# Output projection by seven block products: the large sums of its weights and operands on VectorE instead of GpSimd

## The chip, the cores and the metric

The kernel runs on one core of a Trainium2 chip. The metric is the device time of one execution in microseconds; of several executions the median is taken. The engines are named as in the profile: PE is TensorE (matmuls), DVE is VectorE, ACT is ScalarE, POOL is GpSimd, SP is SyncE, which only issues transfers here. A row of the profile reads: start, duration, engine, line, operation, output<-inputs, shape; in square brackets stands how long the engine idled ahead of it and what ended that.

## What is computed

One layer of a diffusion backbone on 1024 latent tokens of width 1024, with 256 context tokens. All is fp32.

```python
h_lat = rms_norm(x, norm1_g) * (1 + sc1) + sh1          # sh1, sc1, g1, ... from c @ w_mod
h_ctx = rms_norm(ctx, norm1_g) * (1 + csc1) + csh1
# one input projection, columns split into two head groups
(rq, rk, rv, rg), (dq, dk, dv) = split_heads(h @ w_in)
# retention, 4 heads, chunks of 128, in both directions, states carried from chunk to chunk
scores = einsum('bhid,bhjd->bhij', qc, kc) * intra
o = scores @ vc + (qc * q_dec) @ S
S = S * c_dec + (kc * k_dec).T @ vc
y_ret = silu(rg) * (group_norm(o_forward) + group_norm(o_backward))
# differential attention, 4 heads
y_diff = subln((softmax(q1 k1) - lam * softmax(q2 k2)) @ v)
x = x + g1 * (concat(y_ret, y_diff) @ w_out)            # the output projection
h2 = rms_norm(x, norm2_g) * (1 + sc2) + sh2
u = depthwise_conv3(h2 @ w_up) + conv_b
x = x + g2 * ((silu(a) * b) @ w_down)                   # a, b = halves of u
out = rms_norm(x, final_g)
```

## The kernel before

**Matmuls.** Every large product takes each operand as a high and a low part and makes three passes into one PSUM bank: high·high, high·low, low·high (`passes`, L133 to L135). So each operand is cast by ACT (the high part) and then DVE subtracts it from the original (the low part): `split_into` does that at L1333 and L1334, `split_op` at L1246 and L1247.

**What sets the order.** The code is handed to a scheduler that orders each engine's instructions by its own estimates; each engine then works strictly in that order. `in_order` pins stretches to the written order, and `tc.issue_after(i)` keeps an instruction behind instruction `i`. Work beside a product is written as a generator: `tick()`, called after each three matmuls, draws from `side` and from `along` at a given rate, starting at a given due value.

**Retention.** Beside the last columns of the input projection, `states_before` carries the backward states `Sb` from chunk to chunk (PSUM tile `pub`, DVE L249), and then `outputs()` takes 32 steps forward. A step makes the scores `sc`, the output `po` on PE (from `sc` and the states `Sf` and `Sb`), a copy `o` and its sums of squares `ss` on ACT, the power -0.5 of `ss` on POOL (L119, `rsqrt`), the product `o<-o,ss,gn` on DVE (L309), `y` from it on POOL (L311, L312), a turn of `y` on PE, and the next state `Sf` on DVE (L249). The PSUM tiles of these steps share three buffers (`pst`). `weight_blocks` runs along with it, one piece at a time: for each of four block columns `c` it loads two blocks of `w_out` (`w0x`, `w1x`, or the second half of the tile of `g1`, which the profile calls `g`), multiplies them by the gate `g1`, makes `t1` and a difference, and stores `t1_d`, `w2_d` and `w13_d` in DRAM (the tiles t1d, w2d, w13d of the profile).

**Attention.** Units of one head and one block of queries; a unit's keys `ks`, queries `qhl` and values `va` are loaded by POOL's queue. `first_weights` runs beside it: it loads gated weights (`woraw`) and retention outputs (`s<-yrd`, `y11o`) for the projection's first products.

**Output projection.** A product of 2 x 2 blocks by seven block products (Strassen's kind, with shared sums). Banks `oc`, `os`, `of` take products of four rows `r`, each of twelve matmuls (`out_product`); `to_x1` adds a bank to the residual `x1` on DVE (the tiles `x`, L1330). `oc` is used again on top of what it holds, so the next product into it must wait until DVE has read it. The operands: `t2 = w22 - t1` (L1360), `s2 += a` (L1372), `w21 -= t2` (L1377), each in pieces of 128x512 on POOL, and then `t2o`, `w22o`, `s1o`, `t1o`, ... as split operands. The sums `s2 += a` stand behind the last attention unit.

**After it.** `norm2` scales the rows `x1` (ACT square L1278, power on POOL, DVE scaling L1280); `turned` transposes them on PE (`pt`, L1286) for the up-projection, whose first weights are summed in place by `sums_in_place` (L1310 to L1312) on POOL, for two pairs of weights.

Of the kernel before, what the change touches and what calls it, by code (L numbers as in the profile page):

```python
# [8 lines left out]
F32 = mybir.dt.float32  # L9
# [3 lines left out]
ALU = mybir.AluOpType  # L13
# [46 lines left out]

TAIL = 2
GAP = 128
PREP_RATE, PREP_DUE = 0.4, -8.0
SPARE = (16, 4)
MOD_TICKS = 7
FIRST_LOADS = (22, 23, 25, 26, 28, 30)
# [5 lines left out]
def r32(ap):  # L72
    return ap.bitcast(F32)
# [3 lines left out]
def kernel(  # L77
# [16 lines left out]
    nc = tc.nc  # L94
# [22 lines left out]
    def rsqrt(out_ap, in_ap, mul, eps, n):  # L117
        nc.vector.tensor_scalar(out=out_ap, in0=in_ap, scalar1=mul, scalar2=eps, op0=ALU.mult, op1=ALU.add)
        return nc.gpsimd.tensor_tensor(out=out_ap, in0=out_ap, in1=mhalf[:, :n], op=ALU.pow).ins  # L119
# [29 lines left out]
    yr_d = [dr.tile([P, H, 2, 512], F32, name="yrd0"), dr.tile([P, H, 512], F32, name="yrd1")]  # L149
    t1_d = [dr.tile([P, 512], F32, name=f"t1d{c}") for c in range(4)]  # L150
# [9 lines left out]
    with ExitStack() as p1:  # L160
# [3 lines left out]
        raws = ExitStack()  # L164
# [77 lines left out]
        def dv_row(c):  # L242
            return dv_d[c * P : (c + 1) * P, :].rearrange("p (h e) -> p h e", e=P)

        def state_step(dst, prev, pu, h, d):
            if prev is None:
                nc.vector.tensor_copy(dst, pu)
            else:
                nc.vector.scalar_tensor_tensor(out=dst, in0=prev, scalar=cd[:, d * H + h : d * H + h + 1], in1=pu, op0=ALU.mult, op1=ALU.add)  # L249

        def load_step(n):
            h, t = divmod(n, NT)
# [161 lines left out]
        def weight_blocks():  # L414
            shared = rp.tile([P, 2, 2, 512], F32, name="g1", tag="rtab")
            g1 = shared[:, 0]
            nc.sync.dma_start(out=g1.rearrange("p n e -> p (n e)"), in_=g1_d)
            blocks = {}

            def load(c, i):  # L420
                t = blocks[c, i] = shared[:, 1] if c % 2 > i else er.tile([P, 2, 512], F32, name=f"w{i}x", tag="xhl")
                (nc.sync if c + i < 2 else nc.gpsimd).dma_start(out=t, in_=w_out[:, :, 4 * i + c, :].rearrange("n p e -> p n e"))

            def gated(t):
                nc.gpsimd.tensor_tensor(out=t, in0=t, in1=g1, op=ALU.mult)

            def kept(dst, o):
                nc.gpsimd.dma_start(out=dst, in_=o)

            load(0, 0)  # L430
            load(0, 1)
            for c in range(4):
                wa, wb = blocks[c, 0], blocks[c, 1]
                yield
                gated(wa)
                if c == 0:
                    load(1, 0)
                yield
                gated(wb)
                kept(w2_d[c], wb)  # L440
                yield
                t1 = er.tile([P, 512], F32, name="t1", tag=("xa", "xb")[c % 2])
                nc.gpsimd.tensor_tensor(out=t1, in0=wa[:, 1, :], in1=wa[:, 0, :], op=ALU.subtract)
                kept(t1_d[c], t1)
                yield
                nc.gpsimd.tensor_tensor(out=wa[:, 1, :], in0=wb[:, 1, :], in1=wa[:, 1, :], op=ALU.subtract)
                kept(w13_d[c], wa)
                for n, i in ((c + 1, 1), (c + 2, 0)):
                    if n < 4:
                        load(n, i)  # L450

        def natural(wget, lhs, tiles, finish):
            for t in tiles:
# [145 lines left out]
        with ExitStack() as p0:  # L599
# [70 lines left out]
            wget, load = stream_parts(2)  # L670
# [149 lines left out]
        er = p1.enter_context(tc.tile_pool(name="er", bufs=2, reuse_waits="tile"))  # L820
# [7 lines left out]
        cd = rc.tile([P, 8], F32, name="cd")  # L828
# [107 lines left out]
        n_units = NT * H  # L936
        units = {}
# [225 lines left out]
    raw_tiles = {}  # L1163

    def yraw(n, k):
        key = n, k // 2
        if key not in raw_tiles:
            raw_tiles[key] = opp.tile([P, 2, 512], F32, name=f"{n}{k // 2}", tag=f"r{PLACES[n] + k // 2}")
        return raw_tiles[key][:, k % 2, :]

    opb, later = {}, []
    u_ops, v_ops, a_ops = {}, {}, {}

    def first_weights():
        srcs = [(u_ops, "u", c, w13_d[c][:, 0, :]) for c in range(4)] + [(v_ops, "v", c, w2_d[c][:, 0, :]) for c in range(4)]
        raws = []
        for i in range(len(srcs) + 3):
            k = i // 2
            if i < len(srcs):
                if i % 4 == 0:  # L1180
                    yraw("s3", k)
                    nc.sync.dma_start(out=raw_tiles["s3", k // 2], in_=yr_d[1][:, k : k + 2])
                if i % 2 == 0:
                    a_ops[k] = op_tile("a", k, "y11o")
                    nc.gpsimd.dma_start(out=a_ops[k], in_=yr_d[0][:, k])
                raws.append(wrp.tile([P, 512], F32, name="woraw"))
                nc.sync.dma_start(out=raws[i], in_=srcs[i][3])
            if i >= 4 and i % 2 == 0:
                s3 = yraw("s3", k - 2)
                for a in range(2):  # L1190
                    part = r32(a_ops[k - 2][:, a, :])
                    later.append(dict(out=s3, in0=(part, s3)[a], in1=(s3, part)[a], op=(ALU.subtract, ALU.add)[a]))
            if i >= 3:
                ops, tag, c, _ = srcs[i - 3]
                o = ops[c] = op_tile(tag, c)
                nc.scalar.copy(o[:, 0, :], raws[i - 3])
                later.append(dict(out=o[:, 1, :], in0=raws[i - 3], in1=r32(o[:, 0, :]), op=ALU.subtract))
            yield
# [68 lines left out]
    x1 = [(x1lp if t < 4 else x1hp).tile([P, D], F32, name=f"x1_{t}") for t in range(NT)]  # L1267
    raw0 = rwp.tile([P, KD, 512], F32, name="raw0")
    sm2 = rwp.tile([P, 64], F32, name="sm2")

    def x1_load(ts):
        for t in ts:
            nc.sync.dma_start(out=x1[t], in_=x[t * P : (t + 1) * P, :])

    def norm2(t):
        nc.sync.dma_start(out=x1_d[t], in_=x1[t])
        sq = xo.tile([P, D], BF16, name="sq2")
        nc.scalar.activation(sq, x1[t], AF.Square, accum_out=sm2[:, t : t + 1])  # L1278
        power = rsqrt(sm2[:, t : t + 1], sm2[:, t : t + 1], 1.0 / D, EPS, 1)
        nc.vector.tensor_scalar(out=x1[t], in0=x1[t], scalar1=sm2[:, t : t + 1], scalar2=None, op0=ALU.mult)  # L1280
        return power

    def turned(hf, d, raw, on_act):
        pt = turn_tile[0]()
# [22 lines left out]
    def sums_in_place(a, b):  # L1307

        a1, a2, b1, b2 = a[:, 0:4, :], a[:, 4:8, :], b[:, 0:4, :], b[:, 4:8, :]
        nc.gpsimd.tensor_tensor(out=b1, in0=b1, in1=b2, op=ALU.add)  # L1310
        nc.gpsimd.tensor_tensor(out=a1, in0=b1, in1=a1, op=ALU.subtract)
        nc.gpsimd.tensor_tensor(out=a2, in0=a2, in1=a1, op=ALU.subtract)  # L1312

    C = 512
    left, right = slice(0, C), slice(C, D)
    with ExitStack() as p3:
# [25 lines left out]
        def raw_sums(n, tag):  # L1342
            o = [wop.tile([P, C], F32, name=n, tag=tag) for _ in range(4)]
            for k in range(4):
                nc.sync.dma_start(out=o[k], in_=dict(t1=t1_d[k], t3=w13_d[k][:, 1, :], w21=w2_d[k][:, 0, :], w22=w2_d[k][:, 1, :])[n])
            return o
# [9 lines left out]
        w22raw, t1raw = raw_sums("w22", "whi"), raw_sums("t1", "wlo")  # L1356
        x1_load(range(4))
        t2raw = [wop.tile([P, C], F32, name="t2", tag=("whi", "wlo")[k % 2]) for k in range(4)]
        for k in range(4):
            nc.gpsimd.tensor_tensor(out=t2raw[k], in0=w22raw[k], in1=t1raw[k], op=ALU.subtract)  # L1360
        chain = [psr.tile([P, C], F32, name=f"oc{r}", tag=f"c{r}") for r in (3, 0, 1, 2)]
        chain = chain[1:] + chain[:1]
        for r in range(4):
# [2 lines left out]
        with tc.issue_after(units[n_units - 1].exp_ins):  # L1366
            s2o = c_ops("s2")
        t2o = split_all("u", "t2o", t2raw)
        with tc.issue_after(units[n_units - 1].pool_ins.ins):
            for k in range(4):  # L1370
                for a in range(2):
                    nc.gpsimd.tensor_tensor(out=yraw("s2", k), in0=yraw("s2", k), in1=r32(a_ops[k][:, a, :]), op=ALU.add)  # L1372
        x1_load(range(4, NT))
        w22o = split_all("w", "w22o", w22raw)
        w21raw = raw_sums("w21", "whi")
        for k in range(4):
            nc.gpsimd.tensor_tensor(out=w21raw[k], in0=w21raw[k], in1=t2raw[k], op=ALU.subtract)  # L1377
        other = others("os")
        for r in range(4):
            out_product(other[r], r, opb, v_ops, True)  # L1380
# [29 lines left out]
        raws = [up_load(j) for j in range(NSUM)]  # L1410
# [106 lines left out]
    with ExitStack() as p4:  # L1517
# [143 lines left out]
        b0, b1 = Block(0), Block(1)  # L1661
# [16 lines left out]
        b2 = Block(2)  # L1678
# [30 lines left out]
        for j in range(3, NF):  # L1709
# [9 lines left out]
            last = blk  # L1719
# [32 lines left out]
    with ExitStack() as p5:  # L1752
# [255 lines left out]
```

## Time and profile before

| | |
|---|---|
| median of 3 runs | 1402.94 us (1401.28 to 1404.97) |
| profiled execution, its own time | 1398.59 us |
| its span | 1396.8 us |
| mean granted TensorE clock | 0.993 |
| PE busy | 1358.8 us (97%), 6980 matmuls |
| DVE busy | 1040.1 us (74%), 1492 instructions |
| ACT busy | 756.9 us (54%) |
| POOL busy | 434.3 us (31%), 445 instructions |

The span is the time from the first to the last instruction that the profile holds. A busy share is an average over stages that differ much; what an engine costs is read from the waits of a stage. A released wait is written as "PE oc L133 <- DVE x L1330": PE, about to write `oc`, waited for DVE's instruction on `x`.

### The profile page before, as it was taken

The numbers are of one execution on the slowest core, as the hardware profiler recorded it, in microseconds if no ns is written. First come the engines' busy times: TensorE is split into PE (matmuls) and PEld (weight loads), VectorE is DVE, ScalarE is ACT, GpSimd is POOL, SyncE is SP. The second block draws the span as 40 slices with busy tenths as digits, with TensorE's granted clock in tenths as the row PEclk, the third lists the DMA queues.
The fourth block names the chain that finished last, engine by engine and source line by source line (L and its number), as shares of the span: only waits on it lengthen the run. The fifth ranks groups of instructions, "written<-read, shape, count | busy, mean of one in ns | idle before, by whom it ended". The sixth has DMA issues, their size and how long they took to land.

```text
span 1396.8 us, 19720 instructions
## 1 busy us (share of the span) xinstructions
PE 1358.8 (97%) x6980; PEld 1139.5 (82%) x6980; DVE 1040.1 (74%) x1492; ACT 756.9 (54%) x1446; POOL 434.3 (31%) x445
## 2 busy tenths in 40 slices
PE   8999999999999899999899999999999999999997
PEld 6788888887888789998687878888888888788886
DVE  5867756634467888886778998887778777898756
ACT  5546444312466789997346745555445555455533
POOL 1310001566446334532704254223332220043003
PEclk9999999999999999999999999999999999999999
DMA  9467987898668494521514223322323226953324
GB/s 385 154 209 246 314 262 241 270 364 300 214 215 217 123 262 100 92 53 44 193 66 166 91 106 113 114 104 100 114 98 114 103 74 224 377 187 110 124 98 151
DMA packets 111242, 240.59 MB, mean 172 GB/s; under 512 B 10084, under 2 KB 42340, under 8 KB 109736
## 3 DMA queue, kind: packets, MB, share of 16 engines
q1 hardware_dynamic: 101320, 209.97, 44.0%
q0 software_dynamic: 9680, 29.10, 8.5%
q8 instruction: 55, 0.90, 0.3%
q14 instruction: 43, 0.35, 0.1%
q10 hardware_dynamic: 144, 0.26, 0.1%
HBM read 170.62 MB, written 68.42 MB: 171 GB/s over the span
## 4 chain that ended last, share of the span: by engine, by line
PE 59%; DMA 4%; DVE 3%; POOL 2%; issue 1%; ACT 1%; SPq 0%; POOLq 0%; DVEq 0%; ACTq 0%
PE chain L133 6%; PE chain L134 6%; PE chain L135 6%; PE pA L953 4%; PE pv L985 4%; PE c L135 4%; PE c L134 4%; PE c L133 4%; PE third L133 3%; PE third L134 3%; PE third L135 3%; PE pt L973 2%; DMA W<-w_down 2%; PE second L135 1%; PE second L134 1%; PE second L133 1%
## 5 line engine op out<-in xcount | busy, mean ns | idle before, releaser
L133 PE MATMUL pl<-hT,whi 128*128 128x512 f32 x256 | 107.6, 420 | 0.0
L1481 POOL TENSOR_TENSOR cmb<-wrb 128x512 f32<-128x512 f32 x20 | 31.1, 1555 | 236.8 <-DMA wrb<-w_up 182.2
L956 DVE TENSOR_REDUCE mt<-pA 128x1 f32<-128x1280 f32 x64 | 95.1, 1489 | 11.0 <-PE pA L953 10.5
L133 PE MATMUL chain<-T,whi 128*128 128x512 f32 x264 | 102.8, 389 | 0.0
L134 PE MATMUL chain<-T,whi 128*128 128x512 f32 x264 | 102.7, 389 | 0.0
L135 PE MATMUL chain<-T,wlo 128*128 128x512 f32 x264 | 102.7, 389 | 0.0
L135 PE MATMUL pl<-hT,wlo 128*128 128x512 f32 x256 | 100.5, 392 | 0.0
L134 PE MATMUL pl<-hT,whi 128*128 128x512 f32 x256 | 100.2, 391 | 0.0
L135 PE MATMUL c<-whi,ghl 128*128 128x512 f32 x232 | 90.4, 390 | 1.2 <-DVE ghl L1769 1.2
L953 PE MATMUL pA<-ks,qhl 128*128 128x512 f32 (+1 forms) x384 | 89.6, 368 | 1.4 <-DMA ks<-dk 1.4
L134 PE MATMUL c<-wlo,ghl 128*128 128x512 f32 x232 | 90.3, 389 | 0.0
L133 PE MATMUL c<-whi,ghl 128*128 128x512 f32 x232 | 90.3, 389 | 0.0
L960 ACT ACTIVATE p<-pA,mt 128x1280 f32<-128x1280 f32 x64 | 85.3, 1333 | 4.6 <-DVE mt L956 4.3
L133 PE MATMUL pn<-whi,hT 128*128 128x512 f32 x192 | 85.7, 446 | 0.2 <-ACT whi L201 0.2
L497 ACT ACTIVATE xb<-pl 32x512 f32<-32x512 f32 (+1 forms) x88 | 52.0, 590 | 61.0 <-PE pl L135 41.7
L1246 ACT CAST whi<-cmb 128x512 fp32r<-128x512 f32 x62 | 38.5, 622 | 77.3 <-PE chain L134 65.7
L953 PEld LDWEIGHTS pA<-ks,qhl 128*128 128x128 f32 x384 | 68.1, 190 | 13.0 <-issue 1.6
L135 PE MATMUL pn<-whi,hT 128*128 128x512 f32 x192 | 76.4, 399 | 1.0 <-POOL hT L662 1.0
L985 PE MATMUL pv<-va,aT 128*128 128x128 f32 x640 | 76.8, 275 | 0.0
L134 PE MATMUL pn<-wlo,hT 128*128 128x512 f32 x192 | 76.0, 396 | 0.8 <-DVE wlo L202 0.8
L985 PEld LDWEIGHTS pv<-va,aT 128*128 128x128 f32 x640 | 74.0, 192 | 0.4 <-ACT aT L979 0.3
L1246 ACT CAST whi<-wra 128x512 fp32r<-128x512 f32 x55 | 33.9, 621 | 70.8 <-PE third L134 43.5
(420 smaller groups left out, 4020.3 us busy)
## 6 DMA issues: line engine op xcount, KB each, us to landing
raw<-w_in SPq DMA_DIRECT2D x32, 512.0 KB, 5.6
wm<-w_mod SPq DMA_DIRECT2D x32, 512.0 KB, 4.8
wra<-w_up SPq DMA_DIRECT2D x24, 512.0 KB, 3.3
wrb<-w_up SPq DMA_DIRECT2D x23, 512.0 KB, 3.4
W<-w_down SPq DMA_DIRECT2D x44, 256.0 KB, 6.1
ad<-s SPq DMA_DIRECT2D x20, 512.0 KB, 3.2
wra<-ad SPq DMA_DIRECT2D x20, 512.0 KB, 3.3
wrb<-ad SPq DMA_DIRECT2D x18, 512.0 KB, 3.4
```

The lines of the kernel that those rows point to most:

```text
L133: mm(ps, lh, rh, start=first, stop=False, skip_group_check=more)
L134: mm(ps, lh, rl, start=False, stop=False, skip_group_check=more)
L135: mm(ps, ll, rh, start=False, stop=last, skip_group_check=more)
L497: nc.scalar.activation(xb[q * blk : (q + 1) * blk, :], pt[o : o + blk, :], AF.Copy, scale=scale)
L953: mm(self.pa[m][:, c0:c1], self.q[:, i, m, qs], self.k[:, m, c0:c1], start=(i == 0), stop=(i == 1))
L956: nc.vector.tensor_reduce(out=self.mt[:, m : m + 1], in_=self.pa[m][:, :LK], axis=AX.X, op=ALU.min)
L960: self.exp_ins = nc.scalar.activation(self.p[m], self.pa[m][:, :LK], AF.Exp, scale=-1.0, bias=self.mt[:, m : m + 1], accum_out=self.s[:, m ...
L973: nc.tensor.transpose(self.pt[g][:, i, :], self.p[0][:, (4 * g + i) * P : (4 * g + i + 1) * P], ident)
L985: mm(self.pv, self.aT[:, c, :], self.v[:, c, :], start=(c == 0), stop=(c == NKT - 1))
L1246: nc.scalar.copy(hi, src)
L1481: nc.gpsimd.tensor_tensor(out=s1, in0=b1, in1=b2, op=ALU.add)
```

## The change

The sums and gates named above go from POOL to DVE: the gating of `w_out` (now in halves of 128x512, each held behind the newest state step by `issue_after(marks["last"])`), `t1` and the difference beside it, `t2`, `s2 += a`, `w21 - t2`, and the in-place sums of the up-projection's weights. The pace of `weight_blocks` goes from 0.4 a tick, from a due value of -8, to 0.22 from -1.5. All loads of `w_out` go on POOL's queue (three were on SP's), in another order: `load(1, 0)` at once, `load(c, 1)` after the first gated half of a column, `load(c + 2, 0)` at a column's end. The ten loads of `first_weights` go from SP's queue to POOL's. The loads of `x1` tiles 4 to 7 are written after those of `w21`. `norm2` returns its scaling instead of its power, so the second `sums_in_place` is held behind the former.

```diff
-PREP_RATE, PREP_DUE = 0.4, -8.0
+PREP_RATE, PREP_DUE = 0.22, -1.5
...
             def load(c, i):
                 t = blocks[c, i] = shared[:, 1] if c % 2 > i else er.tile([P, 2, 512], F32, name=f"w{i}x", tag="xhl")
-                (nc.sync if c + i < 2 else nc.gpsimd).dma_start(out=t, in_=w_out[:, :, 4 * i + c, :].rearrange("n p e -> p n e"))
+                nc.gpsimd.dma_start(out=t, in_=w_out[:, :, 4 * i + c, :].rearrange("n p e -> p n e"))
...
-            def gated(t):
-                nc.gpsimd.tensor_tensor(out=t, in0=t, in1=g1, op=ALU.mult)
+            def gated(t, half):
+                with tc.issue_after(marks["last"]):
+                    nc.vector.tensor_tensor(out=t[:, half, :], in0=t[:, half, :], in1=g1[:, half, :], op=ALU.mult)
...
             load(0, 0)
             load(0, 1)
+            load(1, 0)
             for c in range(4):
...
+                for half in range(2):
+                    yield
+                    gated(wa, half)
+                    if c and not half:
+                        load(c, 1)
+                        wb = blocks[c, 1]
...
-                nc.gpsimd.tensor_tensor(out=t1, in0=wa[:, 1, :], in1=wa[:, 0, :], op=ALU.subtract)
+                with tc.issue_after(marks["last"]):
+                    nc.vector.tensor_tensor(out=t1, in0=wa[:, 1, :], in1=wa[:, 0, :], op=ALU.subtract)
...
-                for n, i in ((c + 1, 1), (c + 2, 0)):
-                    if n < 4:
-                        load(n, i)
+                if c < 2:
+                    load(c + 2, 0)
...
-                    nc.sync.dma_start(out=raw_tiles["s3", k // 2], in_=yr_d[1][:, k : k + 2])
+                    nc.gpsimd.dma_start(out=raw_tiles["s3", k // 2], in_=yr_d[1][:, k : k + 2])
...
-                nc.sync.dma_start(out=raws[i], in_=srcs[i][3])
+                nc.gpsimd.dma_start(out=raws[i], in_=srcs[i][3])
...
-        nc.gpsimd.tensor_tensor(out=b1, in0=b1, in1=b2, op=ALU.add)
-        nc.gpsimd.tensor_tensor(out=a1, in0=b1, in1=a1, op=ALU.subtract)
-        nc.gpsimd.tensor_tensor(out=a2, in0=a2, in1=a1, op=ALU.subtract)
+        nc.vector.tensor_tensor(out=b1, in0=b1, in1=b2, op=ALU.add)
+        nc.vector.tensor_tensor(out=a1, in0=b1, in1=a1, op=ALU.subtract)
+        nc.vector.tensor_tensor(out=a2, in0=a2, in1=a1, op=ALU.subtract)
...
-            nc.gpsimd.tensor_tensor(out=t2raw[k], in0=w22raw[k], in1=t1raw[k], op=ALU.subtract)
+            nc.vector.tensor_tensor(out=t2raw[k], in0=w22raw[k], in1=t1raw[k], op=ALU.subtract)
...
-        with tc.issue_after(units[n_units - 1].pool_ins.ins):
-            for k in range(4):
-                for a in range(2):
-                    nc.gpsimd.tensor_tensor(out=yraw("s2", k), in0=yraw("s2", k), in1=r32(a_ops[k][:, a, :]), op=ALU.add)
-        x1_load(range(4, NT))
+        for k in range(4):
+            for a in range(2):
+                nc.vector.tensor_tensor(out=yraw("s2", k), in0=yraw("s2", k), in1=r32(a_ops[k][:, a, :]), op=ALU.add)
...
+        x1_load(range(4, NT))
         for k in range(4):
-            nc.gpsimd.tensor_tensor(out=w21raw[k], in0=w21raw[k], in1=t2raw[k], op=ALU.subtract)
+            nc.vector.tensor_tensor(out=w21raw[k], in0=w21raw[k], in1=t2raw[k], op=ALU.subtract)
```

How the scheduler's order stands at three places (lines of the changed kernel are its own; a number behind a name tells tiles of one name apart). First POOL's queue at the end of the retention's weight blocks, before:

```order
L422 DMA w1x<-w_out 128x2x512
L443 TENSOR_TENSOR t_2981<-g_2712 128x512
L428 DMA t1d_147<-t_2981 128x512
L425 TENSOR_TENSOR w1x<-w1x,g_2712 128x1024
L428 DMA w2d_155<-w1x 128x1024
L446 TENSOR_TENSOR g_2712<-w1x,g_2712 128x512
L428 DMA w13d_151<-g_2712 128x1024
L119 TENSOR_TENSOR ss<-ss,mhalf 128x2
```

and after:

```order
L424 DMA g_2644<-w_out 128x2x512
L119 TENSOR_TENSOR ss<-ss,mhalf 128x2
L313 TENSOR_TENSOR y<-o 128x128
L314 TENSOR_TENSOR y<-y,kvgf 128x128
L119 TENSOR_TENSOR ss<-ss,mhalf 128x2
L431 DMA w2d_154<-w1x 128x1024
L313 TENSOR_TENSOR y<-o 128x128
L431 DMA w13d_150<-w0x 128x1024
L119 TENSOR_TENSOR ss<-ss,mhalf 128x2
L314 TENSOR_TENSOR y<-y,kvgf 128x128
L424 DMA w1x<-w_out 128x2x512
L313 TENSOR_TENSOR y<-o 128x128
```

Before, the retention's first power `ss` stands behind the last block's gate and difference. After, POOL holds only transfers beside `ss` and `y`, and the last two columns of blocks are spread over the forward steps. DVE's queue at the same place after (the gates L428, and the difference L454, stand between states and steps):

```order
L251 SCALAR_TENSOR_TENSOR Sf<-Sf,cd,puf 128x128
L428 TENSOR_TENSOR w1x<-w1x,g_2644 128x512
L288 TENSOR_TENSOR sc<-pc_3149,dec 128x256
L118 TENSOR_SCALAR ss<-ss 128x2
L311 SCALAR_TENSOR_TENSOR o<-o,ss,gn 128x128 x2
L251 SCALAR_TENSOR_TENSOR Sf<-Sf,cd,puf 128x128
L118 TENSOR_SCALAR ss<-ss 128x2
L428 TENSOR_TENSOR w1x<-w1x,g_2644 128x512
L288 TENSOR_TENSOR sc<-pc_3189,dec 128x256
L311 SCALAR_TENSOR_TENSOR o<-o,ss,gn 128x128 x2
L454 TENSOR_TENSOR w0x<-w1x,w0x 128x512
L251 SCALAR_TENSOR_TENSOR Sf<-Sf,cd,puf 128x128
```

Before, only the steps' own rows stood there; a gate that waits for its block now holds up the rows behind it. Next, DVE's queue in the output projection, from the first `t2o`, before:

```order
L1334 TENSOR_TENSOR t2o_7159<-t_7083,t2o_7159 128x512
L1334 TENSOR_TENSOR s1o_7275<-s_5496,s1o_7275 128x512
L1334 TENSOR_TENSOR t2o_7160<-t_7084,t2o_7160 128x512
L1334 TENSOR_TENSOR t2o_7161<-t_7085,t2o_7161 128x512
L1334 TENSOR_TENSOR s1o_7276<-s_5496,s1o_7276 128x512
L1330 TENSOR_TENSOR x_0_7045<-oc_7092,x_0_7045 128x512
L1334 TENSOR_TENSOR t2o_7162<-t_7086,t2o_7162 128x512
```

and after:

```order
L1366 TENSOR_TENSOR t_7093<-w_7073,t_7081 128x512
L1366 TENSOR_TENSOR t_7094<-w_7074,t_7082 128x512
L1340 TENSOR_TENSOR t2o_7167<-t_7091,t2o_7167 128x512
L1340 TENSOR_TENSOR t2o_7168<-t_7092,t2o_7168 128x512
L1336 TENSOR_TENSOR x_0_7053<-oc_7100,x_0_7053 128x512
L1340 TENSOR_TENSOR t2o_7169<-t_7093,t2o_7169 128x512
L1336 TENSOR_TENSOR x_1_7054<-oc_7101,x_1_7054 128x512
L1340 TENSOR_TENSOR t2o_7170<-t_7094,t2o_7170 128x512
L1340 TENSOR_TENSOR w22o_7190<-w_7074,w22o_7190 128x512
L1336 TENSOR_TENSOR x_2_7055<-oc_7102,x_2_7055 128x512
```

The sums `t` (L1366) now stand in DVE's own queue, and `x` of `oc` (L1336) moved ahead of the third `t2o` and of all `s1o`; the `w` sums (L1382) follow behind, ahead of `t1o` and `s1o`. Last, DVE's queue where the rows of `norm2` end, before:

```order
L1330 TENSOR_TENSOR x_6_7051<-oc_7094,x_6_7051 128x512
L1280 TENSOR_SCALAR x_4_7049<-x_4_7049,sm_7054 128x1024
L118 TENSOR_SCALAR sm_7054<-sm_7054 128x1
L1280 TENSOR_SCALAR x_5_7050<-x_5_7050,sm_7054 128x1024
L1247 TENSOR_TENSOR wlo<-wrb,whi 128x512
L1280 TENSOR_SCALAR x_6_7051<-x_6_7051,sm_7054 128x1024
L1435 TENSOR_TENSOR raw_7053<-r_7844,raw_7053 128x512
```

and after:

```order
L1254 TENSOR_TENSOR wlo<-wrb,whi 128x512
L1287 TENSOR_SCALAR x_5_7058<-x_5_7058,sm_7062 128x1024
L1287 TENSOR_SCALAR x_6_7059<-x_6_7059,sm_7062 128x1024
L1316 TENSOR_TENSOR wrb<-wrb 128x512
L1473 TENSOR_TENSOR ua<-second,ua 128x512
L1317 TENSOR_TENSOR wra<-wrb,wra 128x512
L1440 TENSOR_TENSOR raw_7061<-r_7852,raw_7061 128x512
L1318 TENSOR_TENSOR wra<-wra 128x512
```

The second set of in-place sums (L1316 to L1318) comes right behind the last scaling, between the first sums of the up-projection; the first set stands further ahead, between the splits and the scaling of `x_7`.

More of the change, by code (lines that the diff above doesn't have):

```diff
@@ L243, in dv_row @@
             return dv_d[c * P : (c + 1) * P, :].rearrange("p (h e) -> p h e", e=P)
+        marks = {}
         def state_step(dst, prev, pu, h, d):
             if prev is None:
-                nc.vector.tensor_copy(dst, pu)
+                marks["last"] = nc.vector.tensor_copy(dst, pu).ins
             else:
-                nc.vector.scalar_tensor_tensor(out=dst, in0=prev, scalar=cd[:, d * H + h : d * H + h + 1], in1=pu, op0=ALU.mult, op1=ALU.add)
+                marks["last"] = nc.vector.scalar_tensor_tensor(out=dst, in0=prev, scalar=cd[:, d * H + h : d * H + h + 1], in1=pu, op0=ALU.mult, op1=ALU.add).ins
         def load_step(n):
@@ L431, in weight_blocks @@
             load(0, 1)
+            load(1, 0)
             for c in range(4):
-                wa, wb = blocks[c, 0], blocks[c, 1]
-                yield
[L435 to L439, printed above, removed]
+                wa, wb = blocks[c, 0], blocks.get((c, 1))
+                for half in range(2):
[4 more added lines that the diff above has]
+                        wb = blocks[c, 1]
+                yield
+                t1 = er.tile([P, 512], F32, name="t1", tag=("xa", "xb")[c % 2])
+                with tc.issue_after(marks["last"]):
+                    nc.vector.tensor_tensor(out=t1, in0=wa[:, 1, :], in1=wa[:, 0, :], op=ALU.subtract)
+                kept(t1_d[c], t1)
+                for half in range(2):
+                    yield
+                    gated(wb, half)
                 kept(w2_d[c], wb)
                 yield
-                t1 = er.tile([P, 512], F32, name="t1", tag=("xa", "xb")[c % 2])
-                nc.gpsimd.tensor_tensor(out=t1, in0=wa[:, 1, :], in1=wa[:, 0, :], op=ALU.subtract)
-                kept(t1_d[c], t1)
-                yield
-                nc.gpsimd.tensor_tensor(out=wa[:, 1, :], in0=wb[:, 1, :], in1=wa[:, 1, :], op=ALU.subtract)
+                nc.vector.tensor_tensor(out=wa[:, 1, :], in0=wb[:, 1, :], in1=wa[:, 1, :], op=ALU.subtract)
                 kept(w13_d[c], wa)
-                for n, i in ((c + 1, 1), (c + 2, 0)):
-                    if n < 4:
-                        load(n, i)
+                if c < 2:
+                    load(c + 2, 0)
         def natural(wget, lhs, tiles, finish):
@@ L1278, in norm2 @@
         nc.scalar.activation(sq, x1[t], AF.Square, accum_out=sm2[:, t : t + 1])
-        power = rsqrt(sm2[:, t : t + 1], sm2[:, t : t + 1], 1.0 / D, EPS, 1)
-        nc.vector.tensor_scalar(out=x1[t], in0=x1[t], scalar1=sm2[:, t : t + 1], scalar2=None, op0=ALU.mult)
-        return power
+        rsqrt(sm2[:, t : t + 1], sm2[:, t : t + 1], 1.0 / D, EPS, 1)
+        return nc.vector.tensor_scalar(out=x1[t], in0=x1[t], scalar1=sm2[:, t : t + 1], scalar2=None, op0=ALU.mult).ins
     def turned(hf, d, raw, on_act):
```

## Prediction

> **What bounds the kernel now.** I read the busy times of the page first, then TensorE's own list of waits, and then the time around each wait it names, by engine. Line numbers are those of the kernel before; "the first, second, third and fourth place" below are the stretches at 344, 507, 687 and 753 us of its trace.
>
> ```profile
> PE 1358.8 (97%) x6980; PEld 1139.5 (82%) x6980; DVE 1040.1 (74%) x1492; ACT 756.9 (54%) x1446; POOL 434.3 (31%) x445
> ```
>
> TensorE is the bound: 1396.8 − 1358.8 leaves 38 us without a matmul. The change removes no matmul and adds none, so it can win only part of these 38 us and the slow clock behind some of them. These are the waits in its reach:
>
> ```profile
> PE oc L133 <- DVE x L1330: 6.5, 1, 6.5
> PE pt L1286 <- DVE x L1280: 2.7, 2, 1.5
> ...
> PE pA L953 <- DMA ks<-dk: 1.4, 1, 1.4
> ```
>
> The columns are us in total, times, and the longest. Next, a table of stretches (start:end, length, then busy time of PE, PEld, DVE, ACT, POOL, then TensorE's granted clock, DMA share, GB/s):
>
> ```profile
> 270.00:345.00 75.00, 71.98 (x365) 60.10 (x363) 27.07 (x54) 14.83 (x27) 43.25 (x37) 1.00 0.99 347
> 343.00:348.00 5.00, 2.81 (x12) 2.53 (x13) 2.21 (x8) 1.18 (x5) 3.37 (x7) 0.80 0.52 206
> 348.00:353.00 5.00, 5.00 (x29) 4.33 (x27) 2.00 (x8) 1.45 (x6) 2.03 (x5) 0.86 0.59 168
> 488.00:508.00 20.00, 18.64 (x137) 16.82 (x135) 17.48 (x21) 17.67 (x43) 8.27 (x18) 1.00 1.22 286
> 750.00:760.00 10.00, 7.29 (x29) 5.47 (x28) 7.68 (x9) 4.80 (x9) 9.25 (x8) 0.83 0.22 90
> 760.00:834.00 74.00, 72.69 (x333) 59.93 (x332) 72.31 (x92) 46.88 (x76) 23.51 (x13) 1.00 0.25 90
> ```
>
> In the retention (270 to 345) POOL is the busiest helper and DVE idles 48 of 75 us. From 760 to 834 DVE has no time left (72.3 of 74), so nothing may be pushed into that stretch.
>
> **First place: gating beside the retention.** POOL's rows, then DVE's, then TensorE's:
>
> ```profile
> 338.04 2.37 POOL L425 TENSOR_TENSOR w1x<-w1x,g 128x1024 f32<-128x1024 f32 x1 [3.72 <-DMA w1x<-w_out]
> ...
> 343.49 0.73 POOL L119 TENSOR_TENSOR ss<-ss,mhalf 128x2 f32<-128x2 f32 x1
> ...
> 338.98 1.45 DVE L118 TENSOR_SCALAR ss<-ss 128x2 f32<-128x2 f32 x1
> 344.26 0.61 DVE L309 SCALAR_TENSOR_TENSOR o<-o,ss,gn 128x128 f32<-128x128 f32 x2 [3.83 <-POOL ss L119]
> ...
> 345.19 0.49 PE L292 MATMUL po<-Sf,qk 128*128 128x128 f32 x2 [2.25 <-DVE Sf L249]
> ```
>
> The last weight block holds POOL from 338.04 until 343.49. The power for `ss`, whose input DVE had done by 340.43, stands behind it; DVE's `o` waits 3.83 for that power, the next state `Sf` stands behind `o`, and TensorE idles 2.25. Then the clock is down: (1 − 0.80) × 5 + (1 − 0.86) × 5 = 1.7 us. After the change POOL has only transfers there, and the power runs at once: **−3.9 us** (2.2 + 1.7).
>
> The price is 16 gates of halves, 4 `t1` and 4 `w13` sums on DVE. A sum of 128x512 alone takes 0.60 from start to start (rows of the third place), so 24 × 0.60 = 14.4 us of DVE in its 48 idle us. What could make them cost is not their length but what DVE and POOL must wait for in order:
>
> ```profile
> POOL w1x L425 <- DMA w1x<-w_out: 9.1, 3, 3.7
> POOL w0x L425 <- DMA w0x<-w_out: 8.3, 1, 8.3
> POOL w1x L422 <- DMA w2d<-w1x: 7.2, 3, 5.0
> ...
> DVE Sb L249 <- PE pub L362: 26.1, 26, 1.3
> ...
> DVE Sf L249 <- PE puf L303: 12.5, 12, 1.9
> ```
>
> The first two are gates waiting for landings, on POOL, where nothing else stood. Now DVE waits, with the states `Sb` or `Sf` behind it, and through them TensorE. DVE waits for TensorE at nearly every state (up to 1.3 and 1.9 us), so a delay below some 1.5 us is swallowed. The third row, a reload that waits until its buffer is stored, stays on POOL's queue, but some of these now have `ss` and `y` behind them. The bounds are 0 and all of 9.1 + 8.3 + 7.2 = 24.6 us; nothing here can go below 0, since the gain is counted already. The slower pace of the gating (0.22 a tick for 0.4) gives landings more time and `w1x` of a new block is asked for earlier than used, so I take the low end: **+2**.
>
> **Second place: ten loads from SyncE's queue to POOL's.**
>
> ```profile
> 491.17 16.75 DMA ks<-dk
> ...
> woraw<-w13d SPq DMA_DIRECT2D x4, 256.0 KB, 13.2
> ...
> L428 POOL DMA_DIRECT2D w2d<-w1x x4 | 2.3, 578 | 0.6 <-POOL w1x L425 0.6
> ```
>
> The keys `ks` of the next attention head take 16.75 us to land while the two `s` and eight `woraw` loads share the DMA engines (share 1.22 from 488 to 508). Now those ten stand behind `ks` in POOL's queue, so `ks` lands earlier by more than the 1.35 us TensorE waited: **−1.4**. POOL issues ten more, 10 × 0.58 = 5.8 us, of its 11.7 idle us in that stretch: between 0 and 5.8, and 0 is the nearer, since one issue delays the small power that may stand behind it by 0.58 only.
>
> **Third place: the output projection.** The groups are of DVE from 662 to 692 (busy us, mean ns):
>
> ```profile
> 662.57 3.77 POOL L1372 TENSOR_TENSOR s<-s,y11o 128x512 f32<-128x512 f32 x3
> ...
> 677.30 5.92 POOL L1360 TENSOR_TENSOR t<-w,t 128x512 f32<-128x512 f32 x4
> ...
> 688.73 0.68 DVE L1330 TENSOR_TENSOR x<-oc,x 128x512 f32<-128x512 f32 x1
> 689.33 0.68 DVE L1330 TENSOR_TENSOR x<-os,x 128x512 f32<-128x512 f32 x1
> ...
> 680.74 0.39 PE L134 MATMUL os<-opv,opb 128*128 128x512 f32 x1
> 680.97 0.39 PE L135 MATMUL os<-opv,opb 128*128 128x512 f32 x1
> 687.87 0.76 PE L133 MATMUL oc<-t2o,s 128*128 128x512 f32 x1 [6.51 <-DVE x L1330]
> ...
> 690.57 0.46 PE L133 MATMUL oc<-t2o,s 128*128 128x512 f32 x1
> ...
> L1334 DVE TENSOR_TENSOR w22o<-w,w22o 128x512 fp32r<-128x512 f32 x4 | 6.9, 1775 | 0.0
> L1334 DVE TENSOR_TENSOR t2o<-t,t2o 128x512 fp32r<-128x512 f32 x4 | 5.7, 1445 | 3.1 <-ACT t2o L1333 3.1
> L1334 DVE TENSOR_TENSOR s1o<-s,s1o 128x512 fp32r<-128x512 f32 x4 | 4.9, 1219 | 0.0
> ```
>
> POOL begins its sums at 662.57 and comes to `t` only at 677.30; DVE's low halves of `t2o` follow it, and in DVE's order three of them stand ahead of the sum `x<-oc` that frees the bank: 6.51 us idle. Six matmuls then take 690.57 − 687.87 = 2.70 instead of 6 × 0.23 = 1.38: 1.3 more. DVE takes over 8 + 4 + 4 sums, 16 × 0.60 = 9.6 us, and gets back 4 × (1.775 + 1.445 + 1.219 − 3 × 0.677) = 9.6 us, since its slow rows ran beside POOL's sums. Its load is unchanged, and it no longer waits for POOL. In the order of DVE after, the fourth `t2o` is the 26th row from the first of these sums, and the last `s1o` the 45th: begun at 662.6, as POOL did, that gives 662.6 + 26 × 0.6 = 678 against 681.2, when TensorE wants it, and 689.6 against 692.1 (four rows `r` of 12 matmuls, 4 × 12 × 0.227 = 10.9, later). Both ahead: **−7.8**. Ends: 0, if the `w21` loads land late, and −7.8.
>
> **Fourth place: sums of the up-projection's weights.**
>
> ```profile
> 741.54 2.38 DVE L1247 TENSOR_TENSOR wlo<-wrb,whi 128x512 fp32r<-128x512 f32 x2
> ...
> 745.22 1.78 DVE L1294 TENSOR_TENSOR B<-raw,B 128x512 fp32r<-128x512 f32 x1
> ...
> 750.74 0.74 DVE L1280 TENSOR_SCALAR x<-x,sm 128x1024 f32<-128x1024 f32 x1
> ...
> 753.83 1.62 DVE L1280 TENSOR_SCALAR x<-x,sm 128x1024 f32<-128x1024 f32 x1
> ...
> 753.22 0.33 PE L1286 MATMUL pt<-ident,x 128*128 128x128 f32 x1 [1.23 <-DVE x L1280]
> ...
> 755.50 0.67 PE L1286 MATMUL pt<-ident,x 128*128 128x128 f32 x2 [1.48 <-DVE x L1280]
> ```
>
> Before the last scaled `x` DVE wins 1.1 (two `wlo`) + 1.1 (`B`) + 0.9 (`x`) = 3.1 us and takes on three sums, 1.8: it is 1.3 earlier, at 754.2. TensorE's order puts that transpose four matmuls later (0.9). Of 2.7 us idle I keep 1.2; the clock's loss, 0.17 × 10 = 1.7, goes: **−3.2**. Ends: −4.4, and +3.6 (all six sums on a DVE without slack). Three more sums come after `x`, 1.8 us, against the 1.3 it is ahead by: DVE enters 760 about half a microsecond late at worst.
>
> The Trainium skill's page "TensorE: Matmul & The Clock Gate" ("What's actually happening") lets the clock fall only after an idle window of about 3.4 us. By that alone the idle times of 2.25 and 1.48 would cost no clock and the sum would be 3.4 us smaller; the clocks of 0.80 and 0.83 right behind them disagree, and I follow the rows.
>
> Costed at nothing: the later `x1_load` (tiles 4 to 7 are used only in the second half of the projection) and the returned scaling of `norm2`, which moves only what may be issued behind it.
>
> **Sum.** −3.9 + 2 − 1.4 − 7.8 − 3.2 = −14.3 in the profiled execution, of which I give back 1.3 for a share of the third place's data being late: −13. That execution took 1398.59 (span 1396.8 and 1.8 around it), 4.35 under the median of 1402.94. I subtract from the median: **1390**. A measurement here tells 0.3%, some 4.2 us, from no change.
>
> **Rivals.**
> - *The retention waits for landings* (the other side). DVE and POOL now wait in order where states stand behind them. For it: 24.6 us of such waits in the rows above. Against it: slack of 1.3 to 1.9 us in nearly every step, and the three PSUM buffers that `pst` turns over. It decides when more than 16.3 us (the gains) of the 24.6 reach TensorE. With all: 1402.9 − 16.3 + 24.6 = 1411. The skill's page "SBUF — State Buffer" ("Who interferes with whom") says that transfers from GpSimd's queue starve for descriptors while DVE holds the shared port in its two-port modes; that would push this rival, and the ten loads. No run here shows it. Chance 0.11.
> - *The third place's wait moves on* to `t1o` and `s1o`: DVE's four `w21` sums stand ahead of them and wait for loads issued only when `w22o` is done. For it: 2.5 us of margin by my row count. Half of the gain returned: +4, 1394. Chance 0.18.
> - *The fourth place's DVE becomes the bound*: its gain of 3.2 lost, and 3.6 more at the wait near 834: +6.8, 1397. For it: 72.3 of 74 busy. Against: 3.1 won before. Chance 0.1.
> - *Nothing moves*: the waits are replaced by others of like size, 1403. For it: the schedule is rewritten at all four places at once. Chance 0.11.
>
> **Numbers.** The forecast has 0.5 (1384 to 1393). Faster by over 0.3%: the forecast, the second rival, and most of the third: 0.77. Same: the fourth and a bit of the third, 0.13. Slower: 0.10. The range of 8 in 10 is 1383 to 1402: below, all gains and no new wait (1402.9 − 16.3 = 1386.6) and 3.6 more, since the execution itself was seen 4.4 under its median; above, the rivals that leave no gain.
>
> **What the profile after would show.** Right: TensorE's waits `oc` on `x` and `po` on `Sf` at 344 gone, `pt` on `x` near 1, no `pA` on `ks` at 507, `w22o`, `t2o` and `s1o` near 0.68 us each, the clock at 1.00 at all four places. Wrong: new TensorE waits on `Sb`, `Sf` or `po` between 280 and 390 with DVE or POOL waiting for `w_out`, `w2d` or `w13d`; a wait on `t1o` or `s1o`; a longer wait near 834.

## The result, and the profile after

The changed kernel takes 1387.22 us (median) where the kernel before takes 1402.11: a ratio of 0.989, 95% interval 0.9865 to 0.9915. The prediction said 1390. Two further sets of runs of the same kernel gave 1387.65 (0.9901, 0.9883 to 0.992) and 1387.26 (0.9911, 0.9896 to 0.9925). One of the first four runs was disturbed (6385 us, its matmuls several times slower throughout; without it the median is 1386.96), and it was the profiled one; the profile shown here is of the second set, called "the changed kernel" below. Its span is 1385.6.

The busy times and TensorE's list of waits (us in total, times, longest):

```profile
PE 1357.6 (98%) x6980; PEld 1139.7 (82%) x6980; DVE 1050.2 (76%) x1538; ACT 757.4 (55%) x1446; POOL 381.7 (28%) x420
```

```profile
PE pyt L318 <- ACT o L296: 3.5, 1, 3.5
...
PE pt L980 <- ACT aT L986: 1.9, 3, 0.7
...
PE third L133 <- DVE ub L1611: 1.6, 1, 1.6
...
PE pt L1292 <- DVE x L1287: 1.1, 1, 1.1
...
PE pub L364 <- DVE Sb L251: 0.7, 1, 0.7
```

The 6.5 us on `oc`, the 1.4 us on `ks` and the 2.2 us on `Sf` at 344 are gone, and `pt` waits 1.1 instead of 2.7. Two waits are new: 3.5 us on ACT's copy `o` (L296), and 0.7 us on `Sb`. The stretches (columns as in the prediction: busy time of PE, PEld, DVE, ACT, POOL, TensorE's clock, DMA share, GB/s):

```profile
270.00:345.00 75.00, 74.31 (x381) 62.63 (x380) 35.57 (x77) 16.59 (x30) 15.23 (x22) 1.00 0.93 317
345.00:405.00 60.00, 56.54 (x338) 49.76 (x337) 32.39 (x97) 27.73 (x103) 31.85 (x53) 0.94 0.76 251
...
662.00:692.00 30.00, 29.52 (x131) 24.10 (x130) 26.00 (x44) 14.13 (x27) 3.14 (x3) 1.00 0.71 252
...
740.00:760.00 20.00, 18.95 (x99) 15.39 (x99) 18.05 (x30) 15.89 (x28) 5.49 (x5) 1.00 0.20 80
```

From 270 to 345 TensorE idles 0.7 us where it idled 3.0. From 662 to 692 it idles 0.5, and the clock is full there and from 740 to 760. But from 345 to 405 it idles 3.5, with the clock down to 0.94. In the output projection DVE's rows are short again (busy us, mean ns, from 662 to 692), and the product into `oc` follows `os` without a gap:

```profile
L1340 DVE TENSOR_TENSOR w22o<-w,w22o 128x512 fp32r<-128x512 f32 x4 | 2.7, 680 | 0.0
...
L1340 DVE TENSOR_TENSOR t2o<-t,t2o 128x512 fp32r<-128x512 f32 x4 | 2.6, 678 | 0.0
...
L1340 DVE TENSOR_TENSOR s1o<-s,s1o 128x512 fp32r<-128x512 f32 x4 | 2.5, 678 | 0.0
```

```profile
681.25 0.39 PE L135 MATMUL os<-opv,opb 128*128 128x512 f32 x1
681.48 0.39 PE L133 MATMUL oc<-t2o,s 128*128 128x512 f32 x1
```

Where the 3.5 us come from is read from three engines around 386 to 395 us: POOL's load of the rope table, SyncE's load of a block of `w_in`, ACT's cast of that block, and TensorE:

```profile
385.30 0.62 POOL L231 DMA_DIRECT2D rtab<-rope  x1 [1.08 <-DMA w13d<-g]
...
386.35 0.33 SPq L194 DMA_DIRECT2D raw<-w_in  x1
...
393.70 1.04 ACT L201 CAST whi<-raw 128x1024 fp32r<-128x1024 f32 x1 [5.33 <-DMA raw<-w_in]
394.65 0.37 ACT L296 COPY o<-po 128x256 f32<-128x256 f32 x1
...
395.16 0.45 PE L318 MATMUL pyt<-ident,y 128*128 128x128 f32 x1 [3.46 <-ACT o L296]
395.26 0.77 PE L133 MATMUL pl<-hT,whi 128*128 128x512 f32 x1
395.83 0.63 PE L134 MATMUL pl<-hT,whi 128*128 128x512 f32 x1
396.26 0.63 PE L135 MATMUL pl<-hT,wlo 128*128 128x512 f32 x1
```

`rtab` takes the buffer of the gate `g1`, so its load waits until the last gated block is stored. With the slower pace of the gating that is at 385, not at 372.5 as before. It carries 1 MB and begins 1.05 us ahead of `raw` (512 KB). ACT's cast of `raw`, which waits for the landing, begins 7.3 us after the issue, and the copy `o` stands behind that cast in ACT's order. In the kernel before the cast began 4.1 us after the issue:

```profile
372.52 0.62 POOL L231 DMA_DIRECT2D rtab<-rope  x1
...
389.27 0.33 SPq L194 DMA_DIRECT2D raw<-w_in  x1
...
393.40 1.05 ACT L201 CAST whi<-raw 128x1024 fp32r<-128x1024 f32 x1 [2.11 <-DMA raw<-w_in]
```

Counted from the first `pub` of each trace (275.14 and 273.33), the block is asked for 4.7 us sooner than before, but its cast begins only 1.5 us sooner, and the slow clock behind the wait takes that too: what the gating had won was gone here.

### The profile page after: what moved, and what is told of

The parts are those of the page before. It is cut to its first block, busy times and chain, and to the rows that moved or that the text cites. A ratio compares the mean times of both kernels' runs of the same rounds, so it can differ in the third digit from the quotient of the medians.

```text
span 6383.6 us, 19720 instructions
## 1 busy us (share of the span) xinstructions
PE 6374.1 (100%) x6980; PEld 4288.9 (67%) x6980; DVE 1035.3 (16%) x1538; ACT 781.0 (12%) x1446; POOL 343.9 (5%) x420
## 4 chain that ended last, share of the span: by engine, by line
PE 100%; DVE 0%; ACT 0%; POOLq 0%; issue 0%; POOL 0%; ACTq 0%
PE pv L992 7%; PE pA L960 7%; PE pl L133 5%; PE pl L135 5%; PE pl L134 5%; PE pn L133 5%; PE pn L134 5%; PE pn L135 5%; PE chain L134 5%; PE chain L133 5%; PE chain L135 4%; PE c L134 4%; PE c L133 4%; PE c L135 4%; PE pt L980 3%; PE third L133 2%
## 5 line engine op out<-in xcount | busy, mean ns | idle before, releaser
L960 PE MATMUL pA<-ks,qhl 128*128 128x512 f32 (+1 forms) x384 | 472.0, 1540 | 0.0
L133 PE MATMUL pl<-hT,whi 128*128 128x512 f32 x256 | 470.2, 1837 | 0.0
L992 PEld LDWEIGHTS pv<-va,aT 128*128 128x128 f32 x640 | 432.6, 942 | 6.0 <-issue 5.2
L992 PE MATMUL pv<-va,aT 128*128 128x128 f32 x640 | 435.3, 1046 | 0.0
L135 PE MATMUL pl<-hT,wlo 128*128 128x512 f32 x256 | 433.5, 1693 | 0.0
L134 PE MATMUL pl<-hT,whi 128*128 128x512 f32 x256 | 431.5, 1685 | 0.0
L133 PE MATMUL pn<-whi,hT 128*128 128x512 f32 x192 | 369.0, 1922 | 0.0
L135 PE MATMUL pn<-whi,hT 128*128 128x512 f32 x192 | 324.3, 1691 | 0.0
L133 PEld LDWEIGHTS pl<-hT,whi 128*128 128x128 f32 x256 | 237.9, 929 | 85.2 <-issue 85.2
L134 PEld LDWEIGHTS pl<-hT,whi 128*128 128x128 f32 x256 | 237.5, 928 | 79.2 <-issue 79.2
L134 PE MATMUL chain<-T,whi 128*128 128x512 f32 x264 | 290.3, 1100 | 0.0
L133 PE MATMUL chain<-T,whi 128*128 128x512 f32 x264 | 289.9, 1098 | 0.0
L133 PE MATMUL c<-whi,ghl 128*128 128x512 f32 x232 | 255.1, 1100 | 0.0
L135 PE MATMUL c<-whi,ghl 128*128 128x512 f32 x232 | 251.9, 1086 | 0.0
L135 PEld LDWEIGHTS pn<-whi,hT 128*128 128x128 f32 x192 | 174.8, 910 | 76.7 <-issue 76.7
L133 PEld LDWEIGHTS pn<-whi,hT 128*128 128x128 f32 x192 | 175.2, 912 | 56.2 <-issue 56.2
```

The source lines that it names most:

```text
L133: mm(ps, lh, rh, start=first, stop=False, skip_group_check=more)
L134: mm(ps, lh, rl, start=False, stop=False, skip_group_check=more)
L135: mm(ps, ll, rh, start=False, stop=last, skip_group_check=more)
L960: mm(self.pa[m][:, c0:c1], self.q[:, i, m, qs], self.k[:, m, c0:c1], start=(i == 0), stop=(i == 1))
L992: mm(self.pv, self.aT[:, c, :], self.v[:, c, :], start=(c == 0), stop=(c == NKT - 1))
```

## The experiments

Each kernel below was timed in five rounds against the kernel before on the same chip; the chips differ from kernel to kernel, so a difference of a microsecond or two between kernels is read from the traces as well. In the first group one place of the change is taken back, or made alone; the order of the other instructions stays as it is, but for a few rows around the fourth place where that one is taken back.

**Again, and the four places one by one.** The changed kernel unedited:

> The changed kernel once more, for a profile of an undisturbed execution and a closer time. The prediction's account: 13 to 15 us under the kernel before; no wait of TensorE on x before oc (6.5 us before), about 1.2 us of pt on x left, no pA on ks at 507, and no po on Sf at 344. The rival with landings: new waits of TensorE on Sb, Sf or po between 280 and 390 us, and a gain made elsewhere.

1387.65 us; its profile is the one above. All four readings came out, and the rival's new waits are there too, in part: 0.7 on `Sb`, and the 3.5 us, which is no wait for `w_out`.

The gating back on GpSimd, with `t1` and the difference, the pace and the loads of `w_out` as before (two places of the edit):

```diff
-                    nc.vector.tensor_tensor(out=t[:, half, :], in0=t[:, half, :], in1=g1[:, half, :], op=ALU.mult)
+                nc.gpsimd.tensor_tensor(out=t, in0=t, in1=g1, op=ALU.mult)
...
-PREP_RATE, PREP_DUE = 0.22, -1.5
+PREP_RATE, PREP_DUE = 0.4, -8.0
```

> The changed kernel with the gating put back as before (on GpSimd in whole blocks, the old pace, three w_out loads on SyncE's queue); the sums of the projection stay on VectorE. The prediction: the first place gains 3.9 and gives back 2, so this is 1.9 us slower than the changed kernel, up to 3.9 if no landing costs anything. The rival with landings: the same time or faster than the changed kernel, since the waits for w_out leave VectorE's queue.

1388.39 us (0.9908, 0.989 to 0.9926): 0.7 us over the changed kernel, less than these times can tell apart. TensorE's two longest waits from 270 to 405:

```profile
PE pn L134 <- DVE wlo L202: 2.4, 1, 2.4
PE pn L133 <- ACT whi L201: 1.1, 1, 1.1
```

The wait on `Sf` at 344 did not come back. TensorE stands 3.5 us at 326 to 329 instead: ACT's cast waits 3.7 us for a block `raw` of `w_in`, and DVE's two `wlo` behind it, beside POOL's sums, take 2.0 us each where one alone takes 1.2. Of the five traces with the gating on GpSimd, that of the kernel before is the only one with the long wait on `Sf`; the other four lose 2.8 to 3.7 us at `wlo` and `whi`. So this stretch loses about 3 us with the gating on GpSimd, but mostly not where the prediction saw it.

How much of the first place is left can be read more closely from the traces than from the medians. TensorE has the same matmuls in the same order from its first `pub` to its first `pA` in all these kernels. They take 180.7 and 181.5 us in two traces of the changed kernel, and 179.7 to 183.0 in the three traces with another place undone. With the gating on GpSimd they take 180.5 here, 180.4 in the kernel before, and 180.7 in that kernel with the third place alone. So nothing of a gain is seen.

The sums of the projection back on GpSimd:

```diff
-            nc.vector.tensor_tensor(out=t2raw[k], in0=w22raw[k], in1=t1raw[k], op=ALU.subtract)
+            nc.gpsimd.tensor_tensor(out=t2raw[k], in0=w22raw[k], in1=t1raw[k], op=ALU.subtract)
```

(likewise `s2 += a` and `w21 - t2`)

> The changed kernel with t2, s2 += a and w21 - t2 back on GpSimd, and the loads of x1 tiles 4 to 7 where they were. The prediction: 7.8 us slower than the changed kernel, with the wait of 6.5 us on x before oc back. The rival that the wait moved on to t1o and s1o: only about 4 us slower.

1395.98 us (0.9966, 0.9957 to 0.9976): 8.3 slower. The wait is back to the tenth, and so are DVE's long rows:

```profile
PE oc L133 <- DVE x L1336: 6.5, 1, 6.5
```

```profile
L1340 DVE TENSOR_TENSOR w22o<-w,w22o 128x512 fp32r<-128x512 f32 x4 | 6.9, 1777 | 0.0
L1340 DVE TENSOR_TENSOR t2o<-t,t2o 128x512 fp32r<-128x512 f32 x4 | 5.7, 1443 | 3.1 <-ACT t2o L1339 3.1
```

The place by itself, in the kernel before:

> The kernel before with only the third place changed (t2, s2 += a and w21 - t2 on VectorE, the later loads of x1). If the places are independent: 7.5 to 8.5 us faster than the kernel before, as much as undoing it costs the changed kernel. Rival, that the gain needs the other places: under 5 us.

1391.57 us (0.9946, 0.9927 to 0.9965), 9.1 under the kernel before. The third place needs none of the others.

The in-place sums back on GpSimd:

```diff
-        nc.vector.tensor_tensor(out=b1, in0=b1, in1=b2, op=ALU.add)
+        nc.gpsimd.tensor_tensor(out=b1, in0=b1, in1=b2, op=ALU.add)
```

(and the two that follow)

> The changed kernel with the in-place sums of the up-projection's weights back on GpSimd and norm2 returning its power. The prediction: 3.2 us slower than the changed kernel, with the two waits pt on x (2.7 us in all) and a granted clock of 0.83 from 750 to 760 back. The rival that VectorE became the bound there: no slower, or up to 3.6 us faster, with a shorter wait near 834 less the shift.

1391.0 us (0.9923, 0.9905 to 0.9942): 3.35 slower. The times alone barely tell that apart; the trace does:

```profile
PE pt L1293 <- DVE x L1287: 2.8, 2, 1.5
...
PE third L133 <- DVE ub L1612: 1.3, 1, 1.3
```

```profile
740.00:760.00 20.00, 17.14 (x78) 13.40 (x77) 15.56 (x22) 10.81 (x20) 10.48 (x10) 0.91 0.20 81
```

The waits on `x` and the slow clock are back. The later wait on `third` is 1.3 here and 1.6 in the changed kernel, but it is 1.6 too in the kernel with the third place alone (above), whose in-place sums are on GpSimd: of the feared 3.6 us on DVE, none is shown.

The ten loads back on SyncE's queue (the two loads of `s` likewise):

```diff
-                nc.gpsimd.dma_start(out=raws[i], in_=srcs[i][3])
+                nc.sync.dma_start(out=raws[i], in_=srcs[i][3])
```

> The changed kernel with the ten loads of first_weights back on SyncE's queue. The prediction: 1.4 us slower, with the wait pA on ks at 507 back. Rival, that the transfer is hidden anyway once the units start earlier: no difference, under 0.5 us.

1389.03 us (0.9921, 0.9902 to 0.9941), 1.4 to 1.8 over the three sets of the changed kernel, and the wait is there:

```profile
PE pA L960 <- DMA ks<-dk: 2.9, 1, 2.9
```

The difference is within the intervals of the times; the traces tell it apart. From the first `pA` to the first `os` TensorE takes 219.4 us here, 214.8 and 214.7 in two traces of the changed kernel, and 216.6 in the kernel before. The 4.6 us are the wait of 2.9 and a granted clock of 0.83 from 506 to 516, (1 − 0.83) × 10 = 1.7.

**What took the gain of the first place.** My theory was the collision of `rtab` with `raw`; the rivals, that `raw` is late of itself, or that the gating's landings bound the stretch. First the load is moved away from the block, to later:

```diff
-        with tc.issue_after(steps[8].pool_ins):
+        with tc.issue_after(steps[14].pool_ins):
             rtab = load_rope(1, nc.gpsimd)
```

> The changed kernel with one number changed: the load of the rope table rtab is held behind step 14 of the retention instead of step 8, so it is issued at about 392 us, after the weight block raw<-w_in (issued at 386.4) has landed. Theory: in the changed kernel rtab (1 MB, issued at 385.3, since its buffer is freed late by the slower gating) shares the DMA engines with raw, which lands at 393.7 instead of about 390.5; ScalarE's cast waits 5.3 us, TensorE idles 3.5 and loses some 1.5 of clock. Without that, 3.5 to 5 us faster than the changed kernel, and rtab still lands at about 400 against its first use at 410.6. Rival: raw is late of itself, or rtab's later landing stalls its first use: no faster, or slower.

1383.26 us (0.9885, 0.9863 to 0.9906). ACT's cast of the block begins 5.2 us after the issue, the table is issued after it, and TensorE's wait on `o` is 1.4:

```profile
385.02 0.33 SPq L194 DMA_DIRECT2D raw<-w_in  x1
...
391.22 0.62 POOL L231 DMA_DIRECT2D rtab<-rope  x1
...
390.25 1.04 ACT L201 CAST whi<-raw 128x1024 fp32r<-128x1024 f32 x1 [3.22 <-DMA raw<-w_in]
```

Beside the changed kernel on one chip:

> The changed kernel a third time, on the same chip as the next kernel, for a direct comparison. Expected 12 to 15 us under the kernel before, with TensorE's wait on ScalarE's copy o near 395 us (3.5 before).

> The changed kernel with the rope table's load behind step 14, beside the changed kernel. Collision theory: 3 to 5 us faster than it. Rival, that the difference seen came from another chip: under 1 us.

1387.26 us for the changed kernel (its wait on `o` was 4.5 us this time) and 1382.76 (0.9881, 0.9863 to 0.9899) with the later table: 4.5 us. In the latter's profile the cast begins 4.3 us after the issue, the wait on `o` is gone, and the clock is full:

```profile
345.00:405.00 60.00, 59.14 (x369) 52.11 (x369) 35.42 (x104) 31.53 (x113) 34.36 (x57) 1.00 0.78 259
```

Then the collision is made in the kernel before, by the same line with step 12:

> The kernel before with the rope table's load held behind step 12 instead of 8: issued at about 387 us, 2.5 us ahead of raw<-w_in, as the changed kernel has it within a microsecond. Theory of the collision: raw lands 2 to 4 us later than its 4.0 after issue, and the kernel is 2 to 5 us slower than the kernel before. Rival: the same time.

1403.12 us (1.0024, 1.001 to 1.0037), 3.7 slower than the kernel before, with 7.3 us from the block's issue to its cast and the same wait:

```profile
386.90 0.62 POOL L231 DMA_DIRECT2D rtab<-rope  x1
...
389.52 0.33 SPq L194 DMA_DIRECT2D raw<-w_in  x1
...
396.82 1.04 ACT L201 CAST whi<-raw 128x1024 fp32r<-128x1024 f32 x1 [5.29 <-DMA raw<-w_in]
...
PE pyt L316 <- ACT o L294: 3.4, 1, 3.4
```

Last a control: the gating on GpSimd, and the table late as well.

> A control: the changed kernel with the gating put back on GpSimd, and the rope table's load behind step 14. There the table was issued at about 372 us at step 8 and collided with nothing, so by the collision theory moving it to step 14 gains nothing: within 1.5 us of 1388.4, and the distance to the changed kernel with the same late load (1382.8) is then what the gating on VectorE is worth by itself, about 5.5 us. Rival, that a late rope load is better whatever the gating: near 1384.

1387.28 us (0.9894, 0.9876 to 0.9913), 1.1 from the 1388.39 with the early table, and 180.3 us from the first `pub` to the first `pA` for 180.5: a late table is not better in itself. So the gating's change is worth 1387.28 − 1382.76 = 4.5 us where nothing collides (4.0 by the other set of the late table). These kernels ran on different chips, but the stretch agrees: 176.6 and 175.3 us in the two traces with the late table, 3.7 and 4.9 under 180.3. The change moved the gating to VectorE and altered its pace and the order of its loads; what of the gain belongs to the engine alone is not shown.

**Finishing the gating earlier** was the other way out of the collision:

```diff
-PREP_RATE, PREP_DUE = 0.22, -1.5
+PREP_RATE, PREP_DUE = 0.25, -1.5
```

> The changed kernel with the pace of the gating at 0.25 a tick for 0.22, so that the last block is stored before step 8 and rtab is issued at about 372 us, as in the kernel before. Theory of the collision: 3.5 to 5 us faster than the changed kernel, unless the tighter gating stalls the retention. Rival, that the gating's landings bound the stretch: slower, with new waits between 280 and 372.

1388.94 us (0.9921, 0.9902 to 0.994): no faster. The collision is gone (the table is issued at 376.9, and the block's cast begins 4.3 us after its issue), but here the rival of the prediction shows itself. DVE's gates wait for landings, and TensorE behind them:

```profile
DVE w1x L428 <- DMA w1x<-w_out: 5.1, 1, 5.1
...
DVE w0x L428 <- DMA w0x<-w_out: 2.8, 1, 2.8
```

```profile
PE pn L134 <- DVE wlo L202: 3.6, 1, 3.6
PE pub L364 <- DVE Sb L251: 2.2, 1, 2.2
```

The 3.6 us are read from DVE's rows: the gate waited 5.10 for its block until 330.49, and the low part `wlo` that TensorE needs stands behind it.

```profile
330.49 0.69 DVE L428 TENSOR_TENSOR w1x<-w1x,g 128x512 f32<-128x512 f32 x1 [5.10 <-DMA w1x<-w_out]
331.10 1.22 DVE L202 TENSOR_TENSOR wlo<-raw,whi 128x1024 fp32r<-128x1024 f32 x1
```

## Why the prediction was right, and where it was not

- **Third place** (−7.8, from which I gave back 1.3): undone, 8.3. The mechanism and the size were right. DVE ended the fourth `t2o` at 676.4 and the last `s1o` at 687.8, where the row count had given 678 and 689.6. Nothing needed giving back: the `w21` sums did not wait, and the rival that the wait moves on did not happen.
- **Fourth place** (−3.2): undone, 3.35. 1.1 us of `pt` were left, for the 1.2 I kept. No price of DVE's lack of slack afterwards is shown: the wait on `third` is 1.3 or 1.6 us with the sums on either engine.
- **Second place** (−1.4): the wait is gone, and the stretch from `pA` to `os` is 1.9 us shorter than in the kernel before. Undone it costs 1.4 to 1.8 by the medians, which do not resolve it, and 4.6 in the trace, where the wait comes back longer and takes the clock with it.
- **First place** (−3.9 + 2 = −1.9): undone, 0.7 by the medians and nothing by the traces, and the step that failed is in here. The gain by itself came out near its size, 4.5 us without a collision for 3.9, but that is in part luck: the wait on `Sf` behind POOL's gate, from which I sized it, is in one of five traces with the gating on GpSimd, and the others lose as much at `wlo` and `whi`. I looked for its price in DVE's and POOL's waits for `w_out`; there it was 0.7 us, on `Sb`. The price that mattered, 4.5 us, was a transfer that I had not listed: `rtab`, which the slower gating moves by 13 us because it takes the gate's buffer. Its own first use was far off and not late, so by its reader it cost nothing; it cost by its neighbour on the DMA engines.
- **The clock.** I followed the rows, which had the clock fall after short idle times. The runs show that the length of an idle time does not decide it alone. At `pt`, 1.23 and 1.48 us were followed by a clock of 0.83 in the kernel before, but 0.91 and 1.48 us left it at 1.00 in the kernel with the third place alone. The 2.25 us at 344 were followed by 0.80, but 2.2 us on `Sb` at the pace of 0.25 left it at 1.00. With the gating back on GpSimd, 0.4 and 1.6 us at `pt` were followed by 0.84 from 740 to 750, although the in-place sums were on VectorE. So the 1.7 us that I counted for the clock at the first and at the fourth place are not lost in every execution; what decides is open.
- **The rival on the other side** was a real mechanism, but not yet at the pace chosen: at 0.22 the gates' blocks had landed in time (in a second trace one gate waited 1.4 us, and TensorE 1.1 on `Sb`), at 0.25 two of them had not, and 5.8 us of new waits took the place of what was won.

That the sum came so near is partly luck: two errors were on opposite sides. The first place gave 0 to 0.7 instead of 1.9, while the give-back of 1.3 on the third was not needed. The four places undone singly add up to 0.7 + 1.6 + 8.3 + 3.4 = 14.0, against 12.9 to 14.9 for the whole.

The best version is the changed kernel with the rope table behind step 14: 1382.8 to 1383.3 us, in all 16 to 18 us under the kernel before.

## What to carry to other kernels

When a buffer is freed later, follow the load that takes it next, and ask not only when its data is needed but what else is on the DMA engines at its new time; a 1 MB load that nobody waits for can hold up a 512 KB load that somebody does. A wait seen in one trace is one way in which a stretch loses its time; in another execution the same load can show at another instruction, so look at a second trace before sizing a term by it. Sums that move off a slow helper engine win twice where the same sums slowed the fast engine's rows beside them, so count the rows that get shorter before fearing the added work. Work that waits for data in order should be paced by its landings: 0.22 and 0.25 a tick differ by 14%, and by a whole wait.

## What the runs showed of the hardware that was not expected

A transfer on one queue (`rtab` on POOL's) held up one on another (`raw` on SyncE's). From the issue of `raw` to its cast it was 4.0 to 5.2 us in the seven traces where `rtab` was not beside it, and 7.3 to 8.4 us in the six where that load of 1 MB began 0.6 to 2.6 us ahead, with the changed kernel's order and with that of the kernel before alike. That `rtab` loses by it too is not shown: it landed in 7.8 to 9.1 us where they met and in 6.0 to 8.3 where they did not. And the ten loads moved to POOL's queue did not suffer there beside a busy DVE (30.7 of 35 us from 486 to 521); the `woraw` loads landed in 2.9 to 9.2 us (median 6.0), where from SyncE's queue, all issued ahead of the attention's own loads, they took 11.2 to 22.6. The issue times differ, so this is no comparison of the queues by themselves, but it shows none of the starving that the prediction named.
